# Gain vectors of the norms: multiplied into the weights at their split, instead of into the tokens

## The chip, the cores and the metric

One core of a Trainium2 chip runs the whole kernel. The metric is device time in microseconds (us) of one launch, lower is better; a measurement is the median of three runs. Times inside a launch come from one execution taken by the hardware profiler, counted from its first instruction.

Engines: PE multiplies matrices (PEld loads its weights), DVE works on vectors, ACT does copies with a scale and function tables, POOL is a second, slower vector engine, SP issues DMA requests. Every engine takes its own instructions strictly in order.

## The reference

One decoder layer on 1024 tokens of width 1024, in float32, with 256 memory tokens. Every RMS norm has a gain vector g:

```
def rms_norm(x, g):
    xf = x.astype(jnp.float32)
    y = xf * lax.rsqrt(jnp.mean(xf * xf, axis=-1, keepdims=True) + EPS)
    return (y * g.astype(jnp.float32)).astype(x.dtype)
...
  h = RMSNorm_pre(x); one combined input projection h @ w_in whose columns are
  partitioned into three head groups:
    A) dilated sliding-window causal attention (8 heads x 64, rotary) ...
    B) short gated convolution  B * conv3(C * v)  (256 channels = 4 groups x 64);
    C) cross-attention into memory tokens (4 heads x 64).
  each group output is RMS-normalised, groups are concatenated, one output
  projection, RMSNorm_post, residual add.  Then squared-ReLU MLP (4*D_MODEL)
  with pre/post RMSNorm and residual add.
```

A norm whose result goes only into a projection can be written in two ways: (x r g) W, or (x r) (g W), where r is the number per token and g is one number per row of W.

## The kernel before

Float32 products on PE are made of three. `split` (L88 to L92) cuts a tile in a high part (an ACT copy, names ending in h) and a low part (what is left, by a subtraction on DVE, or on POOL at L212); `mm3` then multiplies hi·hi (L101), lo·hi (L102) and hi·lo (L103) into one PSUM tile.

**Start, tokens.** Tokens come in 8 tiles of 128, then 2 of memory tokens (n = 0 to 9). For each: `x_sums` squares it on ACT with a running sum, and takes r on DVE (`ms`) and POOL (`rstd`); `x_norm` multiplies by r and by g, which is held on all 128 partitions, in one DVE instruction with two tensor inputs (`norm_to`, L138); `x_turn(n, q)` transposes half a tile on PE (L277) and splits it to hh and hl (mth and mtl for the memory tiles). `raw_mms(n, k0)` makes the products of tile n with two of the eight weight tiles. A block written out by hand (L547 to L640) sets the order of ACT, DVE, POOL and PE here: each tile's transposes stand between the products of the tile before.

**Weights.** `load_w` requests weight columns on SP, and `cut` splits one k tile of 128 rows into wh (ACT, L88) and wl (POOL, L212, or DVE). The weights of w_in come in four sets j = 0 to 3 (128 columns each of query, key and value) of eight k tiles; the set j = 0 lies in tiles named P at the start, its lo parts alternating between DVE and POOL, the others in `wraw` tiles, of which five exist, shared with the tokens. Behind them come the weights for the memory tokens' keys (wm) and values (wv), and later those of the other two groups. Each of them is split inside the stage before the one that uses it. For w_in sets with three column blocks, each request fetches one block for several k tiles.

**Gain loads.** The vector g_pre is fetched once to all partitions as 512 KB on SP in front of the first weights; g_mem and the gains of the three group outputs (g_y) likewise, later.

**Entry into attention (58 to 92 us).** `rope0` and `turn0` finish queries and keys of the first set, wm and wv are cut, the memory tiles are transposed and multiplied, and set j = 1 is cut for the first attention window, whose exponentials (L461) stand at its head. In each window the products of the next set fill PE between the attention's own steps.

**Outputs (403 to 445 us).** `y_norm` normalises the concatenated group outputs, `y_turn` transposes them (L929) and `wo_load` requests and splits the rows of w_out (woraw to oh and ol), the next request when an earlier lo part is done (`wo_low`). Meanwhile PE makes the last products of the convolution (`tail`), whose weights are the last `load_w`; `z`, `yc` and `yco` are its steps on DVE and ACT.

The rest, up to the end, is the MLP (from 560 us on), which the change doesn't touch.

Of the kernel before, what the change touches and what calls it, by code (L numbers as in the profile page):

```python
# [9 lines left out]
F = mybir.dt.float32  # L10
# [35 lines left out]
def hybrid_block(ctx, tc, x, mem, positions, g_pre_mix, g_mem, w_in, w_mem_kv, conv_w, g_attn_out,  # L46
# [40 lines left out]
    def copy(o, i, scale=1.0):  # L87
        nc.scalar.activation(o, i, AF.Copy, scale=scale)  # L88
# [85 lines left out]
    nc.scalar.activation(first, half_neg, AF.Square)  # L174
    cos = ac.tile([128, NS, 32], F, name="cos")
    sin = ac.tile([128, NS, 32], F, name="sin")

# [4 lines left out]
        XT[n] = stage(name="xt")  # L182
        nc.sync.dma_start(XT[n], tokens[n])

    def load_w(src, c0s, width, n_kt, get=None, later=None, engines=None):

        cols = width * len(c0s)
        engines = engines or [nc.gpsimd]
        res = []
        for k0 in range(0, KT, n_kt):  # L190
            if get and k0==0:
                load_gain(0, ac.tile([128, S], F, name="g_pre", tag="bias"), g_pre_mix)
            if get and k0 == KT // 2:
                load_x(1)
                nc.sync.dma_start(pos, positions[0].rearrange("(t p) -> p t", p=128))
                nc.sync.dma_start(invf, bass.AP(tensor=invf_in.tensor, offset=invf_in.offset,
                                                ap=[[0, 128], [1, 32]]))
            raw = get() if get else stage(name="wraw")
            rv = raw[:, :n_kt * cols].rearrange("p (k c) -> p k c", k=n_kt)
            for i, c0 in enumerate(c0s):  # L200
                nc.sync.dma_start(rv[:, :, i * width:(i + 1) * width],
                                  src[k0 * 128:(k0 + n_kt) * 128, c0:c0 + width].rearrange(
                                      "(k p) c -> p k c", p=128))
            for k in range(n_kt):
                wt = []
                res.append(wt)

                def cut(rv=rv, k=k, wt=wt, eng=engines[(k0 + k) % len(engines)]):
# [84 lines left out]
    nc.sync.dma_start(ident, ident_in)
    g_tok = {}

    def load_gain(n, dst, src):
        g_tok[n] = dst
        bcast_load(dst, src[0], 1024)
    cuts = []
    wj = load_w_in(0, get=lambda: pp.tile([128, 1024], F, name="P", tag="P", bufs=NP), later=cuts,  # L300
                   engines=[nc.vector, nc.gpsimd])
# [247 lines left out]
    with tc.manual_schedule(engines={ACT, DVE, POOL, PE}):  # L549
        ss = small.tile([128, 2], F, name="ss2", tag="ss2")  # L550
        for q in range(2):
            sumsq(ss[:, q:q + 1], XT[0][:, q * 512:(q + 1) * 512], 512)
        s1 = small.tile([128, 1], F, name="s1", tag="s1")
        nc.vector.tensor_add(s1, ss[:, 0:1], ss[:, 1:2])
        r = rstd(s1, D)
        tab = tables()
        for q in range(2):
            cl = slice(q * 512, (q + 1) * 512)
            norm_to(XT[0][:, cl], XT[0][:, cl], g_tok[0][:, cl], r)
        cuts.pop(0)()  # L560
        x_turn(0, 0)
        cuts.pop(0)()
        x_turn(0, 1)
        x_sums(1)
        cuts.pop(0)()
        cuts.pop(0)()
        x_norm(1)
        raw_mms(0, 0)
        cuts.pop(0)()
        cuts.pop(0)()  # L570
        raw_mms(0, 2)
        cuts.pop(0)()
        cuts.pop(0)()
        table_steps(2)
        x_turn(1, 0)
        raw_mms(0, 4)
        x_turn(1, 1)
        load_x(2)
        load_x(3)
        load_x(4)  # L580
        x_sums(2)
        table_steps(2)
        x_norm(2)
        raw_mms(0, 6)
        x_sums(3)
        for n in range(1, NS):
            if n + 4 < NS + 2:
                load_x(n + 4)
            if n == 4:
# [274 lines left out]
    g_y = gpool.tile([128, 1024], F, name="gy", tag="gain")  # L864
    bcast_load(g_y[:, 0:512], g_attn_out[0], 512)
    bcast_load(g_y[:, 512:768], g_conv_out[0], 256)
    bcast_load(g_y[:, 768:1024], g_xattn_out[0], 256)
# [7 lines left out]
    def y_norm(st, groups=((0, 512), (512, 256), (768, 256)), get=None):  # L875
# [660 lines left out]
```

## Time and profile before

| what | value |
|---|---|
| median of 3 runs | 1172.41 us (1171.89 to 1172.46) |
| profiled execution, its own time | 1171.13 us |
| its span, first to last instruction | 1169.3 us |
| mean granted clock of PE | 0.991 |
| busy: PE, DVE, ACT, POOL | 1124.3, 785.9, 622.7, 101.2 us |

Busy shares are means over stages that have different limits: PE is busy 96% of the span, so what is left to gain on it is some 45 us, spread over a few places. The time around the span (1171.13 against 1169.3) is launch and end.

### The profile page before, as it was taken

The numbers are of one execution on the slowest core, as the hardware profiler recorded it, in microseconds if no ns is written. First come the engines' busy times: TensorE is split into PE (matmuls) and PEld (weight loads), VectorE is DVE, ScalarE is ACT, GpSimd is POOL, SyncE is SP. The second block draws the span as 40 slices with busy tenths as digits, with TensorE's granted clock in tenths as the row PEclk, the third lists the DMA queues.
The fourth block names the chain that finished last, engine by engine and source line by source line (L and its number), as shares of the span: only waits on it lengthen the run. The fifth ranks groups of instructions, "written<-read, shape, count | busy, mean of one in ns | idle before, by whom it ended". The sixth has DMA issues, their size and how long they took to land.

```text
span 1169.3 us, 15898 instructions
## 1 busy us (share of the span) xinstructions
PE 1124.3 (96%) x5776; PEld 958.1 (82%) x5776; DVE 785.9 (67%) x1396; ACT 622.7 (53%) x1180; POOL 101.2 (9%) x129
## 2 busy tenths in 40 slices
PE   5979999999999999999999999999999999999996
PEld 4979989898888878887788888888888888888884
DVE  5977777676767356676866655665695565865776
ACT  5675666666667345554655545555654433434450
POOL 2270110202002021110000000000000000000001
PEclk9989999999999999999999999999999999999998
DMA  7341020100020454342474454445894465432205
GB/s 236 110 113 33 11 59 10 50 11 10 19 73 19 111 188 152 120 150 82 109 224 145 161 171 119 144 164 175 273 318 150 144 230 202 162 108 91 93 34 198
DMA packets 121310, 145.30 MB, mean 124 GB/s; under 512 B 8720, under 2 KB 74896, under 8 KB 121232
## 3 DMA queue, kind: packets, MB, share of 16 engines
q1 hardware_dynamic: 121232, 144.30, 37.8%
q8 instruction: 45, 0.74, 0.3%
q14 instruction: 33, 0.27, 0.1%
HBM read 102.33 MB, written 41.94 MB: 123 GB/s over the span
## 4 chain that ended last, share of the span: by engine, by line
PE 83%; DVE 7%; ACT 3%; DMA 3%; issue 2%; POOL 1%; SPq 1%; DVEq 0%; POOLq 0%; ACTq 0%
PE pt L1421 6%; PE mm L1421 6%; PE sc L1421 6%; PE mm L101 6%; PE mm L103 6%; PE mm L102 6%; PE tp L1421 3%; PE ot L1421 3%; PE sc L1132 2%; PE sc L1134 2%; PE mm L1132 2%; PE sc L1133 2%; PE mm L1134 2%; PE mm L1133 2%; PE pt L472 2%; PE sc L407 2%
## 5 line engine op out<-in xcount | busy, mean ns | idle before, releaser
L88 ACT ACTIVATE op<-fraw 128x1024 fp32r<-128x1024 f32 x56 | 59.3, 1059 | 147.5 <-PE tp L1421 75.7
L92 DVE TENSOR_TENSOR op<-fraw,op 128x1024 fp32r<-128x1024 f32 x56 | 68.5, 1223 | 92.4 <-ACT op L88 92.4
L130 POOL TENSOR_TENSOR rstd<-ms,half_neg 128x1 f32<-128x1 f32 (+2 forms) x43 | 29.4, 683 | 762.7 <-DVE s L1439 590.9
L101 PE MATMUL mm<-wh,hh 128*128 128x384 f32 x256 | 91.3, 356 | 0.8 <-ACT wh L88 0.8
L102 PE MATMUL mm<-wl,hh 128*128 128x384 f32 x256 | 87.2, 341 | 0.6 <-DVE wl L212 0.4
L103 PE MATMUL mm<-wh,hl 128*128 128x384 f32 x256 | 87.2, 341 | 0.0
L1421 PE MATMUL mm<-op 128*128 128x512 f32 x336 | 82.3, 395 | 2.5 <-DVE op L92 2.5
L212 POOL TENSOR_TENSOR wl<-wraw,wh 128x384 fp32r<-128x384 f32 (+1 forms) x62 | 56.5, 938 | 294.7 <-ACT wh L88 247.1
L1421 PE MATMUL pt<-op 128*128 128x512 f32 x336 | 80.7, 389 | 0.0
L1421 PE MATMUL sc<-op 128*128 128x512 f32 x336 | 80.4, 389 | 0.0
L1421 PEld LDWEIGHTS mm<-op 128*128 128x128 f32 x336 | 64.2, 191 | 16.4 <-DVE op L92 2.9
L1421 PEld LDWEIGHTS pt<-op 128*128 128x128 f32 x336 | 63.1, 188 | 13.1
L1421 PEld LDWEIGHTS sc<-op 128*128 128x128 f32 x336 | 63.1, 188 | 13.1
L92 DVE TENSOR_TENSOR tl<-pt,th 128x512 fp32r<-128x512 f32 (+1 forms) x96 | 60.0, 642 | 17.2 <-ACT th L88 16.5
L92 DVE TENSOR_TENSOR op<-r_b,op 128x1024 fp32r<-128x1024 f32 x56 | 68.2, 1218 | 0.8 <-ACT op L88 0.8
L461 ACT ACTIVATE P<-P,m 128x896 f32<-128x896 f32 (+3 forms) x64 | 49.7, 776 | 30.2 <-DVE m L459 29.5
L1116 ACT ACTIVATE ef<-ef 128x512 f32<-128x512 f32 x48 | 30.3, 631 | 63.5 <-DVE ef L1155 34.3
L88 ACT ACTIVATE th<-pt 128x512 fp32r<-128x512 f32 (+1 forms) x96 | 52.3, 560 | 20.0 <-PE pt L472 18.1
L88 ACT ACTIVATE op<-r_b 128x1024 fp32r<-128x1024 f32 x56 | 58.4, 1045 | 3.2 <-issue 3.2
L101 PE MATMUL mm<-hh,wh 128*128 128x512 f32 x128 | 52.0, 406 | 0.0
L103 PE MATMUL mm<-hh,wl 128*128 128x512 f32 x128 | 50.9, 398 | 0.0
L102 PE MATMUL mm<-hl,wh 128*128 128x512 f32 x128 | 50.7, 396 | 0.0
(345 smaller groups left out, 3072.5 us busy)
## 6 DMA issues: line engine op xcount, KB each, us to landing
wuraw<-in_w_up SPq DMA_DIRECT2D x32, 512.0 KB, 4.7
f_s<-ef SPq DMA_DIRECT2D x64, 256.0 KB, 2.1
r_b<-in_w_down SPq DMA_DIRECT2D x32, 512.0 KB, 4.8
fraw<-f_s SPq DMA_DIRECT2D x32, 512.0 KB, 3.7
f_a<-ef SPq DMA_DIRECT2D x48, 256.0 KB, 2.6
fraw<-f_a SPq DMA_DIRECT2D x24, 512.0 KB, 4.0
wraw<-in_w_in SPq DMA_DIRECT2D x60, 128.0 KB, 2.6
woraw<-in_w_out SPq DMA_DIRECT2D x8, 512.0 KB, 3.6
```

The costliest lines, as they stand in the source:

```text
L88: nc.scalar.activation(o, i, AF.Copy, scale=scale)
L92: nc.vector.tensor_sub(lo, src, hi.bitcast(F))
L101: nc.tensor.matmul(o, a_hi, b_hi, start=first, stop=False)
L102: nc.tensor.matmul(o, a_hi, b_lo, start=False, stop=False)
L103: nc.tensor.matmul(o, a_lo, b_hi, start=False, stop=last)
L212: eng.tensor_sub(wt[1][:, :cols], rv[:, k], wt[0][:, :cols].bitcast(F))
L461: nc.scalar.activation(p[:, :nk], p[:, :nk], AF.Exp, scale=-1.0, bias=m, accum_out=den[:, 2 * i + h:2 * i + h + 1])
L1116: nc.scalar.activation(t, t if src is None else src, AF.Relu)
L1132: nc.tensor.matmul(b, w[:, 0, k], th[:, k], start=(k == 0 and not prev), stop=False, skip_group_check=True)
L1133: nc.tensor.matmul(b, w[:, 0, k], tl[:, k], start=False, stop=False, skip_group_check=True)
L1134: nc.tensor.matmul(b, w[:, 1, k], th[:, k], start=False, stop=(k == 3), skip_group_check=True)
L1421: nc.tensor.matmul(b, x[:, k, cl], y[:, k], start=(first and s == 0 and k == 0 and m == 0), stop=(s == NSUB - 1 and k == 1 and m == 2), sk ...
```

## The change

No token is multiplied by a gain any more: `x_norm` and `y_norm` multiply by r alone, in an instruction with one tensor input (`scale_to`). The gain is multiplied into the weights where they are split. For that it is held as [128, 8], one column for each k tile of weights, fetched by requests on ACT's queue. In `cut` with a lo part on DVE, ACT's copy takes the column as its scale, and DVE's instruction multiplies and subtracts. With a lo part on POOL, ACT first scales the raw tile in place, and then copies it: one ACT instruction more per cut, 62 in all. For w_out, `wo_load` does as the DVE form does.

Further: the eight lo parts of the first w_in set are all on DVE, put off to places written out by hand (`lows`); w_in tiles are fetched by one request for each k tile, with its three column blocks; ident goes to ACT's queue; the first token tile's products are made with hi weights for all k (hi·hi and lo·hi), and the eight with wl come at the end; both transposes of tile 1 stand behind them.

```diff
+    def scale_to(t, r):
+        nc.vector.tensor_scalar(t, t, r, None, op0=OP.mult)
...
+        even = len(c0s) == 3 and c0s[2] - c0s[1] == c0s[1] - c0s[0] > 0
...
+            if even:
+                step = c0s[1] - c0s[0]
+                rows = src[k0 * 128:(k0 + n_kt) * 128, :3 * step].rearrange("(k p) (i c) -> p k i c", p=128, i=3)
+                for k in range(n_kt):
+                    nc.sync.dma_start(rv[:, k].rearrange("p (i c) -> p i c", i=3),
+                                      rows[:, k, :, c0s[0]:c0s[0] + width])
...
-                    copy(wt[0][:, :cols], rv[:, k])
-                    eng.tensor_sub(wt[1][:, :cols], rv[:, k], wt[0][:, :cols].bitcast(F))
+                    if eng is nc.gpsimd:
+                        copy(rv[:, k], rv[:, k], g)
+                        copy(wt[0][:, :cols], rv[:, k])
+                        eng.tensor_sub(wt[1][:, :cols], rv[:, k], wt[0][:, :cols].bitcast(F))
+                        return
+                    copy(wt[0][:, :cols], rv[:, k], g)
+
+                    def low():
+                        eng.scalar_tensor_tensor(wt[1][:, :cols], rv[:, k], g, wt[0][:, :cols].bitcast(F),
+                                                 op0=OP.mult, op1=OP.subtract)
...
     def x_norm(n):
-        norm_to(XT[n], XT[n], g_tok[n // NS], RS[n])
+        scale_to(XT[n], RS[n])
...
+            nc.scalar.dma_start(g_tok[n][:, k0:k0 + n_k], src[0].rearrange("(k p) -> p k", p=128))
...
-            mm3(p[:, :384], a, b, wj[k][0], wj[k][1], k == 0, k == KT - 1)
+            if n:
+                mm3(p[:, :384], a, b, wj[k][0], wj[k][1], k == 0, k == KT - 1)
+            else:
+                nc.tensor.matmul(p[:, :384], a, wj[k][0], start=(k == 0), stop=False)
+                nc.tensor.matmul(p[:, :384], b, wj[k][0], start=False, stop=False)
+        if n == 0 and k0 + 2 == KT:
+            for k in range(KT):
+                nc.tensor.matmul(p[:, :384], hh[:, k, st * 128:(st + 1) * 128], wj[k][1], start=False,
+                                 stop=(k == KT - 1))
...
-            norm_to(y[:, e0:e0 + wd], y[:, e0:e0 + wd], g_y[:, e0:e0 + wd], r[:, n:n + 1])
+            scale_to(y[:, e0:e0 + wd], r[:, n:n + 1])
...
-        copy(oh[:, k], raw)
-        lows.append(lambda: lo_part(ol[:, k], raw, oh[:, k]))
+        copy(oh[:, k], raw, gk)
+        lows.append(lambda: lo_part(ol[:, k], raw, oh[:, k], gk))
```

**DVE at the start.** These are DVE's rows from the first square sums on, before:

```order
L127 TENSOR_SCALAR ms<-s_137 128x1
L138 SCALAR_TENSOR_TENSOR xt<-xt,rstd,g_pre 128x512 x2
L212 TENSOR_TENSOR wl<-P,wh 128x384
L92 TENSOR_TENSOR hl<-pt,hh 128x4x128 x2
L127 TENSOR_SCALAR ms<-ss 128x1
L212 TENSOR_TENSOR wl<-P,wh 128x384
L138 SCALAR_TENSOR_TENSOR xt<-xt,rstd,g_pre 128x1024
L212 TENSOR_TENSOR wl<-P,wh 128x384 x2
```

And with the change (gt holds the gain's columns):

```order
L127 TENSOR_SCALAR ms<-s_133 128x1
L141 TENSOR_SCALAR xt<-xt,rstd 128x512 x2
L92 TENSOR_TENSOR hl<-pt,hh 128x4x128
L224 SCALAR_TENSOR_TENSOR wl<-P,gt_104,wh 128x384
L92 TENSOR_TENSOR hl<-pt,hh 128x4x128
L127 TENSOR_SCALAR ms<-ss 128x1
L224 SCALAR_TENSOR_TENSOR wl<-P,gt_104,wh 128x384 x3
L141 TENSOR_SCALAR xt<-xt,rstd 128x1024
L224 SCALAR_TENSOR_TENSOR wl<-P,gt_104,wh 128x384 x4
```

Eight lo parts stand on DVE where four stood, three of them ahead of tile 1's scaling; the token norms have lost their second tensor input.

**ACT at the entry into attention.** Before, around the last two copies of the memory tokens (mth):

```order
L88 ACTIVATE wh<-wraw 128x256 x2
L88 ACTIVATE mth<-pt 128x4x128
L88 ACTIVATE wh<-wraw 128x256 x2
L88 ACTIVATE mth<-pt 128x4x128
L88 ACTIVATE wh<-wraw 128x256 x4
L88 ACTIVATE QK<-sc 64x512 x2
```

With the change (gt_216 are the columns of g_mem, gt_104 those of g_pre):

```order
L88 ACTIVATE wraw<-wraw,gt_216 128x256
L88 ACTIVATE wraw<-wraw,gt_104 128x384
L88 ACTIVATE wh<-wraw 128x256
L88 ACTIVATE wh<-wraw,gt_216 128x256
L88 ACTIVATE mth<-pt 128x4x128
L88 ACTIVATE wraw<-wraw,gt_216 128x256
L88 ACTIVATE wraw<-wraw,gt_104 128x384
L88 ACTIVATE wh<-wraw 128x256
L88 ACTIVATE wraw<-wraw,gt_216 128x256
L88 ACTIVATE wh<-wraw 128x256
```

Between the copies stand scalings of the wm and wv tiles (256 wide) and, ahead of the memory tokens' last copies, already those of set j = 1 (384 wide), which need that set's data.

**ACT at the outputs.** Before, from the convolution's copy z on:

```order
L88 ACTIVATE z<-mm 128x512
L88 ACTIVATE wh<-wraw 128x256 x6
L88 ACTIVATE z<-mm 128x512
L88 ACTIVATE wh<-wraw 128x256 x2
L135 ACTIVATE sq,ssy<-y 128x512
L135 ACTIVATE sq,ssy<-y 128x256
L88 ACTIVATE oh<-woraw 128x1024 x2
```

With the change:

```order
L88 ACTIVATE z<-mm 128x512
L88 ACTIVATE wraw<-wraw,gt_104 128x256 x2
L88 ACTIVATE wh<-wraw 128x256 x2
L88 ACTIVATE wraw<-wraw,gt_104 128x256 x2
L88 ACTIVATE z<-mm 128x512
L88 ACTIVATE wh<-wraw 128x256 x2
L88 ACTIVATE wraw<-wraw,gt_104 128x256 x2
L88 ACTIVATE wh<-wraw 128x256 x2
L88 ACTIVATE wraw<-wraw,gt_104 128x256 x2
L88 ACTIVATE wh<-wraw 128x256 x2
L135 ACTIVATE sq,ssy<-y 128x512
L88 ACTIVATE oh<-woraw,gt_451 128x1024
```

Eight scalings stand between the copies, and the square sums of y behind them. On PE the transposes of y stand 16 products of `tail` in before, 41 in with the change.

## Rows read from the trace of the kernel before

**Rows 1.** Windows: busy time and instructions of each engine, then clock, DMA share, GB/s.
```profile
0.00:9.40 9.40, 0.02 (x1) 0.02 (x1) 1.20 (x5) 2.93 (x6) 0.75 (x5) 1.00 0.71 218
9.40:23.40 14.00, 10.25 (x46) 7.72 (x46) 11.67 (x18) 9.47 (x20) 6.32 (x6) 1.00 0.94 292
23.40:48.60 25.20, 25.16 (x160) 24.89 (x160) 21.48 (x51) 15.39 (x32) 2.70 (x5) 1.00 0.35 114
...
59.50:72.00 12.50, 6.76 (x35) 6.05 (x34) 12.28 (x21) 7.46 (x19) 9.97 (x15) 0.67 0.29 81
72.00:90.00 18.00, 16.72 (x123) 16.31 (x122) 11.35 (x25) 15.22 (x31) 12.50 (x14) 0.94 0.51 136
90.00:160.00 70.00, 67.85 (x470) 65.55 (x468) 49.17 (x136) 42.41 (x92) 7.95 (x8) 1.00 0.13 36
```

**Rows 2.** Waits of PE up to 100 us: in total, times, longest.
```profile
PE pt L277 <- DVE xt L138: 13.9, 4, 9.4
PE mm L102 <- DVE mtl L92: 2.1, 1, 2.1
PE sc L542 <- DVE qk L316: 1.5, 1, 1.5
...
PE pt L277 <- DVE ms L127: 0.6, 1, 0.6
```

**Rows 3.** Timeline of DVE, start: start, duration, idle before and its end.
```profile
5.40 0.15 DVE L127 TENSOR_SCALAR ms<-s 128x1 f32<-128x1 f32 x1
8.57 1.41 DVE L138 SCALAR_TENSOR_TENSOR xt<-xt,rstd,g_pre 128x512 f32<-128x512 f32 x2 [3.02 <-DMA P<-in_w_in]
10.35 0.56 DVE L212 TENSOR_TENSOR wl<-P,wh 128x384 fp32r<-128x384 f32 x1 [0.36 <-ACT wh L88]
...
14.50 2.07 DVE L138 SCALAR_TENSOR_TENSOR xt<-xt,rstd,g_pre 128x1024 f32<-128x1024 f32 x1
```

**Rows 4.** Timeline of SP's queue, ACT and PE at the start.
```profile
2.12 0.43 SPq L110 DMA_DIRECT2D g_pre<-in_g_pre_mix  x1
...
9.80 0.52 ACT L88 ACTIVATE wh<-P 128x384 fp32r<-128x384 f32 x1 [4.62 <-DMA P<-in_w_in]
...
12.43 1.06 ACT L135 ACTIVATE sq<-xt 128x1024 bf16<-128x1024 f32 x1 [0.40 <-DMA xt<-in_x]
...
23.43 0.63 PE L277 MATMUL pt<-ident,xt 128*128 128x128 f32 x4 [1.83 <-DVE xt L138]
```

**Rows 5.** DMA issues up to 60 us: KB, median us to landing.
```profile
g_pre<-in_g_pre_mix SPq DMA_DIRECT2D x1, 512.0 KB, 6.3
...
pos<-in_positions SPq DMA_DIRECT2D x1, 4.0 KB, 4.2
```

**Rows 6.** Groups of DVE up to 100 us, by shape: busy, mean ns.
```profile
L138 DVE SCALAR_TENSOR_TENSOR xt<-xt,rstd,g_pre 128x1024 f32<-128x1024 f32 x7 | 9.7, 1391 | 0.0
...
L245 DVE TENSOR_SCALAR tabI<-tabA 128x256 int32<-128x256 f32 x5 | 1.4, 284 | 0.0
```

**Rows 7.** Timeline of ACT, 58 to 92 us.
```profile
64.08 1.33 ACT L88 ACTIVATE wh<-wraw 128x256 fp32r<-128x256 f32 x4
...
84.42 1.35 ACT L88 ACTIVATE wh<-wraw 128x384 fp32r<-128x384 f32 x3
...
88.13 1.15 ACT L461 ACTIVATE P<-P,m 128x1024 f32<-128x1024 f32 x1
...
91.19 1.06 ACT L88 ACTIVATE th<-pt 128x512 fp32r<-128x512 f32 x2
```

**Rows 8.** Timeline at the outputs: POOL, ACT, PE, DVE.
```profile
408.64 5.67 POOL L212 TENSOR_TENSOR wl<-wraw,wh 128x256 fp32r<-128x256 f32 x8 [45.86 <-PE mm L103]
...
412.05 0.71 ACT L88 ACTIVATE wh<-wraw 128x256 fp32r<-128x256 f32 x2
...
415.82 0.87 PE L929 MATMUL pt<-ident,y 128*128 128x128 f32 x6 [1.56 <-DVE y L138]
...
421.14 0.49 DVE L804 TENSOR_SCALAR yc<-z,taps 128x512 f32<-128x512 f32 x1
```

More of the change, by code (lines that the diff above doesn't have):

```diff
@@ L173, in hybrid_block @@
     first = consts.tile([128, 1], F, name="first")
-    nc.scalar.activation(first, half_neg, AF.Square)
     cos = ac.tile([128, NS, 32], F, name="cos")
@@ L183, in load_x, with load_w @@
         nc.sync.dma_start(XT[n], tokens[n])
-    def load_w(src, c0s, width, n_kt, get=None, later=None, engines=None):
+    def load_w(src, c0s, width, n_kt, get=None, later=None, engines=None, fold=None, lows=None):
+        fold = g_tok[0] if fold is None else fold
+        even = len(c0s) == 3 and c0s[2] - c0s[1] == c0s[1] - c0s[0] > 0
         cols = width * len(c0s)
@@ L190, in load_w @@
         for k0 in range(0, KT, n_kt):
-            if get and k0==0:
-                load_gain(0, ac.tile([128, S], F, name="g_pre", tag="bias"), g_pre_mix)
-            if get and k0 == KT // 2:
+            if get and k0 == n_kt:
                 load_x(1)
-                nc.sync.dma_start(pos, positions[0].rearrange("(t p) -> p t", p=128))
-                nc.sync.dma_start(invf, bass.AP(tensor=invf_in.tensor, offset=invf_in.offset,
-                                                ap=[[0, 128], [1, 32]]))
             raw = get() if get else stage(name="wraw")
             rv = raw[:, :n_kt * cols].rearrange("p (k c) -> p k c", k=n_kt)
-            for i, c0 in enumerate(c0s):
+            if even:
[4 more added lines that the diff above has]
+                                      rows[:, k, :, c0s[0]:c0s[0] + width])
+            for i, c0 in enumerate(c0s if not even else ()):
                 nc.sync.dma_start(rv[:, :, i * width:(i + 1) * width],
@@ L206, in load_w, with cut @@
                 res.append(wt)
-                def cut(rv=rv, k=k, wt=wt, eng=engines[(k0 + k) % len(engines)]):
+                def cut(rv=rv, k=k, wt=wt, eng=engines[(k0 + k) % len(engines)], g=fold[:, k0 + k:k0 + k + 1]):
                     wt.append(pw.tile([128, 384], R, name="wh", tag="wh", bufs=8))
                     wt.append(pw.tile([128, 384], R, name="wl", tag="wl", bufs=8))
-                    copy(wt[0][:, :cols], rv[:, k])
-                    eng.tensor_sub(wt[1][:, :cols], rv[:, k], wt[0][:, :cols].bitcast(F))
+                    if eng is nc.gpsimd:
[7 more added lines that the diff above has]
+                                                 op0=OP.mult, op1=OP.subtract)
+                    if lows is None:
+                        low()
+                    else:
+                        lows.append(low)
                 if later is None:
@@ L290, in hybrid_block, with load_gain @@
     XT[0] = stage(name="xt")
+    g_tok = {}
+    def load_gain(n, rows):
+        g_tok[n] = consts.tile([128, KT], F, name=f"gt{n}")
+        k0 = 0
+        for src in rows:
+            n_k = src.shape[1] // 128
+            nc.scalar.dma_start(g_tok[n][:, k0:k0 + n_k], src[0].rearrange("(k p) -> p k", p=128))
+            k0 += n_k
+    load_gain(0, [g_pre_mix])
+    nc.scalar.dma_start(ident, ident_in)
+    nc.scalar.activation(first, half_neg, AF.Square)
     for q in range(2):
         nc.sync.dma_start(XT[0][:, q * 512:(q + 1) * 512], tokens[0][:, q * 512:(q + 1) * 512])
[L293 to L301, printed above, removed]
+    cuts, lows = [], []
+    wj = load_w_in(0, get=lambda: pp.tile([128, 1024], F, name="P", tag="P", bufs=NP), later=cuts, lows=lows,
+                   engines=[nc.vector])
+    nc.sync.dma_start(pos, positions[0].rearrange("(t p) -> p t", p=128))
+    nc.sync.dma_start(invf, bass.AP(tensor=invf_in.tensor, offset=invf_in.offset, ap=[[0, 128], [1, 32]]))
     QT, VT = {}, {}
@@ L522, in raw_mms @@
             a, b = hh[:, k, st * 128:(st + 1) * 128], hl[:, k, st * 128:(st + 1) * 128]
-            mm3(p[:, :384], a, b, wj[k][0], wj[k][1], k == 0, k == KT - 1)
+            if n:
+                mm3(p[:, :384], a, b, wj[k][0], wj[k][1], k == 0, k == KT - 1)
+            else:
+                nc.tensor.matmul(p[:, :384], a, wj[k][0], start=(k == 0), stop=False)
[4 more added lines that the diff above has]
+                                 stop=(k == KT - 1))
         if k0 + 2 == KT:
@@ L556, in hybrid_block @@
         tab = tables()
[L557 to L564, printed above, removed]
         cuts.pop(0)()
         cuts.pop(0)()
+        for q in range(2):
+            scale_to(XT[0][:, q * 512:(q + 1) * 512], r)
+        x_turn(0, 0)
+        lows.pop(0)()
+        cuts.pop(0)()
+        raw_mms(0, 0)
+        x_turn(0, 1)
+        cuts.pop(0)()
+        raw_mms(0, 2)
+        x_sums(1)
+        lows.pop(0)()
+        lows.pop(0)()
+        cuts.pop(0)()
+        lows.pop(0)()
         x_norm(1)
-        raw_mms(0, 0)
+        cuts.pop(0)()
+        raw_mms(0, 4)
+        lows.pop(0)()
         cuts.pop(0)()
         cuts.pop(0)()
[L571 to L577, printed above, removed]
+        lows.pop(0)()
+        lows.pop(0)()
+        lows.pop(0)()
         load_x(2)
@@ L580, in hybrid_block @@
         load_x(4)
+        load_gain(1, [g_mem])
+        raw_mms(0, 6)
+        x_turn(1, 0)
+        x_turn(1, 1)
+        table_steps(2)
         x_sums(2)
@@ L583, in hybrid_block @@
         x_norm(2)
-        raw_mms(0, 6)
         x_sums(3)
@@ L589, in hybrid_block @@
             if n == 4:
-                load_gain(1, kv.tile([128, S], F, name="g_mem", tag="QK", bufs=NSETS), g_mem)
+                load_gain(2, [g_attn_out, g_conv_out, g_xattn_out])
             if n == 6:
                 cuts = []
-                wm = load_w(w_mem_kv, [0], 256, 4, later=cuts, engines=[nc.gpsimd, nc.gpsimd, nc.gpsimd, nc.vector])
+                wm = load_w(w_mem_kv, [0], 256, 4, later=cuts, engines=[nc.gpsimd, nc.gpsimd, nc.gpsimd, nc.vector],
+                            fold=g_tok[1])
             raw_mms(n, 0)
@@ L630, in hybrid_block @@
         cuts = []
-        wv = load_w(w_mem_kv, [256], 256, 4, later=cuts)
+        wv = load_w(w_mem_kv, [256], 256, 4, later=cuts, fold=g_tok[1])
         turn0(0)
@@ L863, in hybrid_block @@
     w = load_w(w_in, [U0 + 128, B0 + 128], 128, 4)
[L864 to L867, printed above, removed]
     YS, YP, OB, XR = {}, {}, {}, {}
@@ L905, in wo_load @@
         nc.sync.dma_start(raw, w_out[k * 128:(k + 1) * 128])
-        copy(oh[:, k], raw)
-        lows.append(lambda: lo_part(ol[:, k], raw, oh[:, k]))
+        gk = g_tok[2][:, k:k + 1]
+        copy(oh[:, k], raw, gk)
+        lows.append(lambda: lo_part(ol[:, k], raw, oh[:, k], gk))
     def wo_low():
```

## The prediction

> **What bounds the kernel now.** I read the windows first. From 90 us on PE is busy 67.85 of 70 us in an attention window, and before that it is short in three stretches: 0.02 of 9.4 us, 10.25 of 14.0 us up to 23.4, and 6.76 of 12.5 plus 16.72 of 18.0 between 59.5 and 90 [rows 1]. In the same rows the reader sees who is busy there instead: DVE 11.67 of 14.0 before 23.4, DVE 12.28 of 12.5 before 72, and ACT 15.22 of 18.0 behind it. The waits of PE name the instruction: 13.9 us on token norms, 9.4 of them before its first instruction and 1.8 and 2.1 later, then 2.1 on the low part of the memory tokens, 1.5 on a rotation and 0.6 behind `ms` [rows 2, 4]. All of that is DVE. In the first of the late stretches PE was granted 0.67 of its clock on average, a mix of its two levels of 1.2 and 2.4 GHz, after idling for 5.7 us in it [rows 1]; what less idle would give back there I leave in the bounds. So a change that makes DVE's norms cheaper works where PE waits; one that gives ACT more works where ACT has little left between 59.5 and 90.
>
> **The start.** The norm of tile 0 began at 8.57 after 3.02 us of idle, though `ms` was done at 5.55; the row puts the idle down to a DMA on SP's queue [rows 3], and of the norm's operands that is g_pre, requested at 2.12 and 6.3 us under way [rows 4, 5]. Without it r is ready some 0.6 us after `ms`, and two scalings of 512 follow, 0.49 each by the only one-tensor row of that width [rows 8]. The first transposes then start near 7 instead of 9.4. The columns of g are 1024 words of 4 bytes, as pos is, which landed in 4.2 us [rows 5]; issued first, on ACT's queue, they are there by 6, ahead of the first weights.
>
> But 2.4 us at the head are not 2.4 us at 23.4. ACT's first wh waited for P until 9.80, and the square of tile 1 stood at 12.43 behind its own DMA [rows 4]; both move only by what g_pre's 512 KB took of a DMA that is 71 to 94% busy [rows 1], under 2 us, and the squares stand in ACT's order behind three weight copies and two hh. Then DVE: the change takes from it, up to the norm of tile 2, 1.41 + 2.07 + 1.39 = 4.87 us of norms [rows 3, 6] and puts 0.98 + 0.9 + 0.9 there, where 0.9 for a width of 1024 is an estimate that continues 0.284 at 256 and 0.49 at 512 [rows 6, 8]. That is 2.1 less. It adds four low parts that POOL had, 0.56 each [rows 3]: 2.2 more. DVE has the same work as before, in a stretch where it is the busiest engine. I walk the new order with these durations: the last low part of tile 0 near 18, tile 1's transposes done at 19.2, tile 2's norm and first transposes at 22.9 instead of 23.43. **Gain 0.5**; bounds 0.5 lost (the squares of tile 1 late by one more copy) and 1.9 won (the whole 1.83 us wait of the row).
>
> **Up to 59.5.** PE runs without a gap from 23.4 to 48.6, DVE is busy 21.48 of 25.2 [rows 1]. Seven norms of 1.39 become 0.9, so DVE gets ahead, and the one wait of PE behind it, 0.6 at tile 7, goes [rows 2]. **Gain 0.6**, bounds 0 and 1. The gain requests on ACT's queue and the joint w_in requests cost nothing seen here: the first fall in ACT's idle time (15.39 busy of 25.2) and the second move the same bytes; if that cover is gone, a request costs ACT what one costs SP, 0.43 [rows 4].
>
> **Entry into attention.** On DVE three norms fall into its full stretch, each 0.5 shorter: up to 1.5 us earlier for the memory tiles and so for 2.1 + 2.1 + 1.5 of PE's waits [rows 2]. On ACT 14 scalings of 256 and 8 of 384 come in. A copy of these widths goes at 1.33/4 = 0.33 and 1.35/3 = 0.45 [rows 7]. A scale by partition isn't in the trace; the nearest pair is an exponential of 1024 with a bias by partition, 1.15 us [rows 7], against 1.06 for a plain 1024 square [rows 4], so 0.09 more. That makes 14 x 0.42 + 8 x 0.54 = 10.2 us; without the 0.09, 8.2. ACT's idle in 59.5 to 90 is 5.04 + 2.78 = 7.8 [rows 1]. ACT is then full, with 2.4 us left over, and in its strict order set j = 1 is scaled ahead of memory copies and must wait for its data, 0.7 and 1.4 us by my walk. Behind it stand the exponentials and th, 91.19 before [rows 7], on which the first window's products end. PE has cover for part: set j = 1 of weights is for later products, and DVE's 1.5 us come in front. I take **0.8 lost**, between 1.5 won (DVE's part passes through, ACT's surplus hides in the window, where ACT is busy 42.41 of 70) and 4.4 lost (2.4 + 2.1 with nothing won).
>
> One rule of the chip speaks against DVE's part. In the row at 14.50 a norm with two tensor inputs took 2.07 beside POOL, against the mean of 1.39 [rows 3, 6]: 0.7 more, shared reading. The Trainium skill ("SBUF — State Buffer", Who interferes with whom) says more of the new form: a `tensor_scalar` in a two-port mode and GpSimd exclude each other for whole instructions. The trace of before has no 1024-wide scaling beside POOL to show it.
>
> **The other sets.** For j = 2 and 3 eight scalings each, 8 x 0.54 = 4.3 us, fall in windows where ACT is busy 42.41 of 70 and PE idle 2.15 [rows 1]. They can only delay an in-order th by one copy. **0.2 lost**, bounds 0 and 1. Each later weight load has the same cover.
>
> **Outputs.** PE waited 1.56 at 415.82 for the norm of y; that norm stood behind POOL's `rstd`, and this behind eight low parts, 408.64 to 414.31 [rows 8]. Eight scalings of 0.42 come into ACT, 3.4 us, while it waits part of this time for weights; the last copies ended at 412.76 [rows 8], and I get 414.3 and POOL's end 1.6 later. The norm itself gets 0.2 shorter. PE no longer waits there, since the transposes stand 25 products later, 25 x 0.23 (estimate: 5.7 us of cover). But `rstd`, the low parts of w_out and so its next requests, which wait for them in turn, come 1.6 to 3 us later, and yc and yco stand behind them on DVE and ACT. 1.56 won against 2.2 lost: **0.6 lost**, bounds 1.6 won and 3 lost.
>
> **Sum.** -0.5 - 0.6 + 0.8 + 0.2 + 0.6 = +0.5 us, on 1171.13 of the profiled execution: 1171.6. The median of the runs is 1172.41, 1.3 above, so I give 1172.9. A measurement here tells about 0.2%, 2.35 us, from no change; this is **no change**.
>
> **Rivals.** *Faster:* ACT's scalings hide, so that DVE's 1.5 us pass through at the entry, and y's wait is gone without a later one, 1 us won. -0.5 - 0.6 - 1.5 + 0.2 - 1.0 = -3.4: 1169.0. For it: all of PE's waits are on DVE, and ACT's idle of 7.8 is near the 8.2 of scalings without the 0.09. Against: the order puts scalings in front of memory copies. *Slower:* ACT is the bound at the entry. -0.5 - 0.6 + 4.4 + 0.2 + 0.6 = +4.1: 1176.5. It decides from the point where th comes more than 2.5 us later than 91.19 at PE's pace. For it: 10.2 us into 7.8. *The late gain was not what held the start* (weights and squares do): the first term is 0, 1173.4. *Lock:* if each scaling beside POOL waits for one of its low parts, two memory norms cost 0.9 + 0.8 instead of 1.36; DVE loses 0.7 in place of 1.0 won, the sum is +2.2, 1174.6; POOL's row at the entry is busy 9.97 of 12.5 [rows 1], which speaks for it, and the scalings of 256 at a mean of 0.284 [rows 6] against it, though few lay beside POOL's work. That is the rule of the page above.
>
> **Chances.** Forecast 0.36, no gain at the start 0.07, lock 0.06, faster 0.28, slower 0.23. The first three lie within 2.35 us, but for some 0.05 at their ends, which I share out: faster by over 0.2% 0.30, within 0.2% 0.44, slower 0.26. The range leaves out 2 in 10: from a little below the faster rival, 1168.2, to the slower one's 1176.5.
>
> **What would show it.** First transposes near 7, tile 2's near 22.9, and no POOL work of weights before 24. No wait of PE near 49. Norms of 1024 at 0.9; 0.4 would be a faster scaling, above 1.3 beside POOL the lock. Between 59.5 and 90 ACT busy over 29 of 30.5, its scalings at 0.42 and 0.54, and th at 91 to 92. At the outputs POOL's last weight near 416, no wait at the transposes of y, a new one at the convolution's. I am wrong on the faster side if ACT's waits at the entry turn out to be idle time that PE does not miss, and on the slower if the set j = 1 arrives so late that ACT stands still in front of the memory copies.

## The result, and the profile after

The changed kernel took 1180.72 us (median of 4 runs, 1177.71 to 1181.75) against 1172.15 of the kernel before (4 runs): a ratio of 1.0071, 95% interval 1.0051 to 1.009. It is slower by some 8 us, where no change was forecast and the range ended at 1176.5. The profiled execution took 1181.75, with a span of 1179.9 against 1169.3. It is the longest of the four, 1.0 above their median, so its places add up to more than 8 us.

Where the time went is found with the starts of the same instructions in both traces (PE's transposes of tile 2, ACT's first th of the attention, its first exponential of the gathered heads, and its 17th copy yh; us from the span's start):

| kernel | tile 2 | first th | gathered heads | yh, 17th |
|---|---|---|---|---|
| before | 23.4 | 91.2 | 340.5 | 520.1 |
| changed | 25.1 | 94.7 | 347.4 | 531.3 |
| late by | 1.7 | 3.5 | 6.9 | 11.2 |

So four places lose: the start 1.7, the way to the first th 1.8 (2.3 counted from tile 7, where the start's loss had shrunk to 1.2), the windows up to 340 us 3.4, and the outputs 4.3. From there on both kernels run alike, and 0.6 comes back.

These sizes are those of one execution of each kernel. The kernels of the experiments share most of the changed code, so their profiles tell how steady a place is. With the changed start, tile 2 came at 24.3 to 25.8. With all scalings at the entry, the way from tile 7 to the first th took 0.8 to 2.3 longer than before. With the last weights scaled on ACT in the changed order, the outputs lost 4.2 to 5.4. The windows are the uneven place: 3.1 of the lateness arise between 318 and 356 us here, and only 0.7 to 1.1 in five other kernels with the same scalings there.

The windows of the changed kernel, as [rows 1], with three around 337 and at 450 us added:

```profile
9.40:23.40 14.00, 12.01 (x42) 9.57 (x42) 8.46 (x18) 7.87 (x17) 0.85 (x1) 1.00 0.87 238
23.40:48.60 25.20, 23.49 (x150) 23.20 (x151) 19.74 (x53) 14.56 (x30) 3.29 (x6) 1.00 0.33 100
...
59.50:72.00 12.50, 9.06 (x57) 8.16 (x56) 10.52 (x21) 10.29 (x24) 9.17 (x13) 0.86 0.34 105
72.00:90.00 18.00, 15.55 (x105) 13.23 (x104) 11.24 (x25) 16.29 (x35) 8.57 (x12) 1.00 0.23 68
...
330.00:337.20 7.20, 4.96 (x32) 4.12 (x31) 1.79 (x8) 5.10 (x14) 0.00 (x0) 1.00 0.60 164
337.40:340.60 3.20, 3.20 (x17) 3.10 (x16) 0.93 (x4) 2.81 (x8) 0.00 (x0) 0.50 0.00 0
...
450.00:453.20 3.20, 2.63 (x10) 2.26 (x11) 1.67 (x5) 2.24 (x8) 0.36 (x2) 0.50 0.62 243
```

At the entry ACT is busy 26.6 of 30.5 us (22.7 before), DVE has eased, and PE's granted clock is higher than before (0.86 and 1.00 against 0.67 and 0.94). At 337 and 450 PE is granted half its clock, 1.2 GHz, each time with a wait. For the start the clock column reads 1.00 in both kernels, but there products of 384 columns follow each other at 0.32 us up to 18 us, against 0.17 later, so I go by that spacing. The waits of PE, in total, times and longest, beside [rows 2]:

```profile
PE pt L294 <- DVE xt L141: 8.9, 2, 8.0
...
PE pt L970 <- DVE y L141: 4.1, 1, 4.1
PE ot L509 <- ACT th L88: 3.9, 6, 2.2
...
PE pt L294 <- DVE ms L127: 1.8, 1, 1.8
PE mm L102 <- DVE mtl L92: 1.4, 1, 1.4
```

The norms' waits have shrunk from 13.9 to 8.9, but 1.8 for tile 2's norm now stand behind `ms` (0.6 before), so 3.8 are gone. New are 4.1 on the second half of y and 2.2 of the 3.9 on th. The start, on PE and then ACT (answers to [rows 4]):

```profile
8.02 1.12 PE L294 MATMUL pt<-ident,xt 128*128 128x128 f32 x4 [8.02 <-DVE xt L141]
...
17.87 0.52 PE L554 MATMUL mm<-wh,hl 128*128 128x384 f32 x1
18.19 2.31 PE L557 MATMUL mm<-wl,hh 128*128 128x384 f32 x8
20.34 1.03 PE L294 MATMUL pt<-ident,xt 128*128 128x128 f32 x8
...
25.11 0.63 PE L294 MATMUL pt<-ident,xt 128*128 128x128 f32 x4 [1.78 <-DVE ms L127]
```
```profile
5.71 0.63 ACT L135 ACTIVATE sq<-xt 128x512 bf16<-128x512 f32 x1 [1.35 <-DMA xt<-in_x]
...
20.98 1.10 ACT L88 ACTIVATE hh<-pt 128x512 fp32r<-128x512 f32 x2
21.95 1.07 ACT L135 ACTIVATE sq<-xt 128x1024 bf16<-128x1024 f32 x1
```

The transposes of tile 1 stand at 20.34, behind all 24 products of tile 0; ACT's copies of them at 20.98; and behind these, in ACT's order, the square of tile 2 that its norm needs. ACT around 334 us, and PE there:

```profile
333.57 1.13 ACT L88 ACTIVATE wraw<-wraw,gt 128x384 f32<-128x384 f32 x2 [1.62 <-DMA wraw<-in_w_in]
...
335.51 0.62 ACT L88 ACTIVATE wraw<-wraw,gt 128x384 f32<-128x384 f32 x1 [0.43 <-DMA wraw<-in_w_in]
336.15 0.60 ACT L88 ACTIVATE th<-pt 128x512 fp32r<-128x512 f32 x1
```
```profile
336.80 0.39 PE L509 MATMUL ot<-th,V 128*128 128x256 f32 x1 [2.24 <-ACT th L88]
```

ACT waits for the convolution's weights in order to scale them, while the copy th that PE needs stands behind. And the outputs, POOL, ACT, DVE and PE in turn (answers to [rows 8]):

```profile
418.58 4.28 POOL L219 TENSOR_TENSOR wl<-wraw,wh 128x256 fp32r<-128x256 f32 x6 [0.86 <-ACT wh L88]
424.71 0.71 POOL L130 TENSOR_TENSOR rstd<-ms,half_neg 128x2 f32<-128x2 f32 x1 [1.85 <-DVE ms L127]
```
```profile
422.11 1.14 ACT L88 ACTIVATE oh<-woraw,gt 128x1024 fp32r<-128x1024 f32 x1
423.15 0.40 ACT L135 ACTIVATE sq<-y 128x256 bf16<-128x256 f32 x1
...
438.01 1.16 ACT L88 ACTIVATE oh<-woraw,gt 128x1024 fp32r<-128x1024 f32 x1 [6.19 <-DMA woraw<-in_w_out]
```
```profile
423.28 1.28 DVE L94 SCALAR_TENSOR_TENSOR ol<-woraw,gt,oh 128x1024 fp32r<-128x1024 f32 x1 [0.89 <-ACT oh L88]
424.48 0.15 DVE L127 TENSOR_SCALAR ms<-ssy 128x1 f32<-128x1 f32 x1
```
```profile
450.57 0.66 PE L970 MATMUL pt<-ident,y 128*128 128x128 f32 x2 [4.10 <-DVE y L141]
```

POOL's last low part ends at 422.9, in the stage's own time (6.9 us late as a whole) 1.7 later than before; `rstd` stands 3.5 later, the later requests of w_out 3, and the second half of y, which needs the convolution behind them, lets PE wait 4.1 us. It is not POOL that held `rstd`: POOL stood idle for 1.85 us in front of it, waiting for `ms`. On ACT a copy of w_out stood between the two square sums of y, and on DVE the low part of that copy stood ahead of the second `ms`.

### The profile page after: what moved, and what is told of

Read it like the earlier page. It is cut to its first block, busy times and chain, and to the rows that moved or that the text cites. A ratio compares the mean times of both kernels' runs of the same rounds, so it can differ in the third digit from the quotient of the medians.

```text
span 1179.9 us, 15906 instructions
## 1 busy us (share of the span) xinstructions
PE 1132.4 (96%) x5776; PEld 961.6 (81%) x5776; DVE 776.9 (66%) x1400; ACT 654.5 (55%) x1242; POOL 97.1 (8%) x125
## 4 chain that ended last, share of the span: by engine, by line
PE 82%; DVE 6%; ACT 6%; issue 2%; DMA 2%; POOL 1%; SPq 0%; POOLq 0%; ACTq 0%; DVEq 0%
PE pt L1462 6%; PE mm L1462 6%; PE mm L103 6%; PE mm L102 6%; PE mm L101 6%; PE sc L1462 6%; PE tp L1462 3%; PE ot L1462 3%; PE sc L1173 2%; PE mm L1173 2%; PE sc L1174 2%; PE sc L1175 2%; PE mm L1175 2%; PE mm L1174 2%; PE pt L499 2%
## 5 line engine op out<-in xcount | busy, mean ns | idle before, releaser
L101 PE MATMUL mm<-wh,hh 128*128 128x384 f32 x248 | 87.9, 355 | 0.3 <-ACT hh L88 0.3
L102 PE MATMUL mm<-wl,hh 128*128 128x384 f32 x248 | 84.6, 341 | 1.1 <-POOL wl L219 1.1
L103 PE MATMUL mm<-wh,hl 128*128 128x384 f32 x248 | 84.0, 339 | 0.1
```

Of the source, the lines that this page charges most:

```text
L101: nc.tensor.matmul(o, a_hi, b_hi, start=first, stop=False)
L102: nc.tensor.matmul(o, a_hi, b_lo, start=False, stop=False)
L103: nc.tensor.matmul(o, a_lo, b_hi, start=False, stop=last)
```

## The experiments

Each was timed beside the kernel before, and ratios are to it. Theory: ACT's 62 in-place scalings lose the time, at three places, and the start's order the rest. Rivals stand with each.

**No scalings.** Whether ACT's added instructions are the cause at all.

```diff
-                        copy(rv[:, k], rv[:, k], g)
```

> The changed kernel without ACT's 62 in-place scalings (the gain is left out of all weights whose low part is made on POOL; the rest is as changed). Theory 'ACT's scalings': three places of the changed profile lose 2.3 us (entry, 59 to 92), 3.0 us (at 334) and 4.3 us (outputs), all behind these instructions; without them about 1171 to 1172.5, and the start's 1.7 us is all that stays against the kernel before, less what DVE's shorter norms won. Rival 'order and start': the new product order, the request form and the start shift the whole program, and the scalings only fill idle time of an engine that is 55% busy; then 1178 or more.

0.9992 (0.9983 to 1.0001), 1170.83 us. The 62 instructions cost 0.8%; without them the change would have made no difference, and the rival falls. The start stays late (tile 2 at 24.5).

**One place at a time.** The same line is left out for one load of weights (`pre` guards it): the last, the convolution's, and those cut at the entry.

```diff
-    w = load_w(w_in, [U0 + 128, B0 + 128], 128, 4)
+    w = load_w(w_in, [U0 + 128, B0 + 128], 128, 4, pre=False)
```
```diff
-    w = load_w(w_in, [U0, B0, C0 + 128], 128, 2)
+    w = load_w(w_in, [U0, B0, C0 + 128], 128, 2, pre=False)
```
```diff
-                            fold=g_tok[1])
+                            fold=g_tok[1], pre=False)
...
-        wv = load_w(w_mem_kv, [256], 256, 4, later=cuts, fold=g_tok[1])
+        wv = load_w(w_mem_kv, [256], 256, 4, later=cuts, fold=g_tok[1], pre=False)
...
-        wj = load_w_in(j + 1, later=cuts)
+        wj = load_w_in(j + 1, later=cuts, pre=j > 0)
```

> The changed kernel without the eight in-place scalings of the last weights alone (U0 + 128, B0 + 128; their gain is left out). Theory 'ACT's scalings': POOL's low parts end about 3 us sooner in the stage, rstd and the requests of w_out move with them, the wait of 4.1 us at the transposes of y shrinks below 1.5, no drop of PE's clock behind it: 1176 to 1177.5. Rival 'order': y's normalisation stands behind two low parts of w_out on DVE and the transposes stand later in any case; then the wait stays over 3 us and the time at 1179.5 to 1181.5.

> The changed kernel without the in-place scalings of the eight convolution weights at 328 to 340 alone (U0, B0, C0 + 128; their gain is left out). Theory 'ACT waits in order': a scaling waits for its weights' transfer (1.6 and 0.4 us) ahead of the copy th that PE waits for (2.2 us), and PE then runs 3.4 us at half its clock; without it 3 us less, 1177 to 1178.5, no wait of PE over 0.6 there and no lower clock at 337. Rival 'load': it is ACT's added busy time (4.3 us in 12), and half the gain comes; 1179 to 1180.

> The changed kernel without the in-place scalings of wm, wv and the set j = 1, 22 instructions between 59 and 100 us (their gain is left out). Theory 'ACT full': the first th comes 2.3 us sooner against the start, at about 92.4, and the whole is 2 to 2.5 us shorter: 1178 to 1178.8. If DVE's shorter norms pass through as well, 3.5 less: 1177. Rival 'later slack': the stage's gain is given back in the windows, where PE waits for th anyway; 1180 to 1181.

Ratios 1.0033 (1.002 to 1.0046), 1.0044 (1.0031 to 1.0058) and 1.0046 (1.0033 to 1.0058): each place alone gives back 0.25 to 0.4%, together 0.9%, about what all at once gave. The first is clear of the changed kernel's interval; the other two overlap it, so their sizes are rough. Without the last weights' scalings the waits of PE on y are (outputs, total and longest):

```profile
PE pt L971 <- DVE y L141: 1.9, 1, 1.9
PE tp L865 <- DVE yc L859: 1.5, 1, 1.5
```

not 4.1, though not below the 1.5 that I had set, and PE's clock does not drop; `rstd` follows POOL's last low part at once there. Without the convolution's, no wait of PE is left between 300 and 345 us, and between 318 and 356 us 0.9 is gained on the kernel before. Where those scalings stay, the place is milder than in the profile above. Here is the kernel without the last weights' scalings, its wait and its window:

```profile
PE ot L510 <- ACT th L88: 1.4, 1, 1.4
```
```profile
330.00:345.00 15.00, 13.53 (x81) 10.66 (x79) 7.81 (x23) 10.34 (x27) 0.00 (x0) 1.00 0.27 74
```

In five such profiles the wait is 1.2 to 1.6 us, PE keeps its full clock, and 0.7 to 1.1 are lost. The mechanism is the same, the 3.1 is that execution's. Without the entry's, the first th comes at 93.4, of which the start of that execution had 0.6 more than the changed kernel's: 1.9 better.

**A warm PE.** The start showed products at 0.32 us each up to 18 us, against 0.17 at full clock; I took the early start of a PE with little to do for the cause of the 1.7.

```diff
+        warm = pt_bank()
+        for i in range(24):
+            nc.tensor.transpose(warm[:, i % 4 * 128:(i % 4 + 1) * 128], ident, ident)
         x_turn(0, 0)
```

> The changed kernel with 24 transposes of ident into an unused bank on PE ahead of the first token transposes, which nobody reads. In the changed profile PE starts at 8.0, stands still between short pieces of work, and its products of 384 columns follow each other at 0.32 us up to 18 us, against 0.17 from 12.6 us on before. Theory 'clock': with PE busy from about 4.5 us on, the full clock comes before 12, tile 0's products take 0.17, tile 2's first transposes come at 23.4 to 24 instead of 25.1, and the whole is 1 to 2 us shorter: 1179 to 1179.7. Rival 'chain': ACT's and DVE's order sets the start (copies, square of tile 1, low parts), products only get shorter, and tile 2's transposes stay within 0.4 us of 25.1: 1180.3 to 1181.

1.0071 (1.0058 to 1.0083). On PE:

```profile
5.82 4.36 PE L598 MATMUL pt<-ident 128*128 128x128 f32 x24 [5.82 <-DMA ident<-in_ident]
10.01 0.60 PE L294 MATMUL pt<-ident,xt 128*128 128x128 f32 x4
...
12.30 0.34 PE L553 MATMUL mm<-wh,hh 128*128 128x384 f32 x1
12.47 0.34 PE L554 MATMUL mm<-wh,hl 128*128 128x384 f32 x1
...
25.08 0.63 PE L294 MATMUL pt<-ident,xt 128*128 128x128 f32 x4 [1.78 <-DVE ms L127]
```

The products do follow at 0.17, and tile 2 comes at 25.08 all the same; the time is the changed kernel's. So the theory's forecast fell. But the run is no clean test of the clock: the useless transposes kept PE until 10.0, and tile 0's own came 2.0 later than in the changed kernel. What the shorter products won may have gone there.

Other profiles say that PE's pace has a part. The kernel before with only its later low parts on DVE (below) has before's start, the same instructions in the same order. In its profile products stand 0.32 apart up to 19.4, where they stood 0.17 apart before, and tile 2 comes 1.2 later than before's 23.43:

```profile
18.78 0.52 PE L101 MATMUL mm<-wh,hh 128*128 128x384 f32 x1
19.10 0.52 PE L102 MATMUL mm<-wl,hh 128*128 128x384 f32 x1
...
24.66 0.63 PE L277 MATMUL pt<-ident,xt 128*128 128x128 f32 x4 [1.86 <-DVE xt L138]
```

And with the changed start tile 2 comes at 24.3 where the last eight products of tile 0 took 1.76 us, and at 25.8 where they took 2.77. So some of the 1.7 is PE's pace; how much stays open. The next experiment changes the order alone.

**The start's order of before**, with the fold and eight low parts on DVE.

```diff
-        raw_mms(0, 6)
-        x_turn(1, 0)
-        x_turn(1, 1)
+        x_turn(1, 0)
+        raw_mms(0, 4)
+        x_turn(1, 1)
...
+        raw_mms(0, 6)
```

> The changed kernel with the start's order of before (three products for each k, tile 1's transposes between them, each low part at once, all eight on DVE). Theory 'clock': PE's work is denser at its start, so the full clock comes at about 13; but DVE has all eight low parts ahead of tile 1's norm. Tile 2's transposes at 23 to 24.3; the whole 1 to 2 us shorter, 1178.7 to 1179.7. Rival 'the new order is right for these low parts': PE waits for each wl in turn, 25 or later, 1180.5 to 1182.

1.0032 (1.002 to 1.0043): 0.4% better, more than expected. On PE and ACT:

```profile
14.79 1.05 PE L294 MATMUL pt<-ident,xt 128*128 128x128 f32 x4
...
17.43 0.60 PE L294 MATMUL pt<-ident,xt 128*128 128x128 f32 x4
...
21.48 0.63 PE L294 MATMUL pt<-ident,xt 128*128 128x128 f32 x4 [1.37 <-DVE xt L141]
```
```profile
18.59 1.06 ACT L135 ACTIVATE sq<-xt 128x1024 bf16<-128x1024 f32 x1
```

Here, too, the products of 384 run at 0.32 up to 17 us. Tile 1's transposes between them bring the square of tile 2 from 21.95 to 18.59, and tile 2 to 21.48: 3.6 earlier than changed, 2.0 earlier than before.

**Low parts on DVE**, all of them by multiply and subtract: no in-place scaling.

```diff
-        engines = engines or [nc.gpsimd]
+        engines = [nc.vector]
```

> The changed kernel with every low part of weights on DVE (copy with the scale on ACT, multiply and subtract on DVE), so no in-place scaling and nothing on POOL; the result is whole. Theory 'ACT's scalings': ACT has as many instructions as before the change, the three places recover as without scalings, less what DVE's 62 instructions of 0.5 to 0.6 us cost where it is full (at the entry 22 of them, 11 us, into some 8.7 us of idle time): 1172 to 1175. Rival 'any added instruction in order': DVE becomes at the entry and at the outputs what ACT was; 1177 to 1181.

0.9967 (0.9955 to 0.9978), faster than the kernel before, where at best its time was expected. With the edits of the last two experiments together:

> The start's order of before and every low part of weights on DVE, in the changed kernel; the result is whole. Theory 'two separate losses' (tile 1's transposes put behind all of tile 0's products; ACT's scalings): the gains add, 3.6 us of the start on top of what the low parts on DVE gave, a ratio of about 0.9935 to the kernel before, 1164 to 1165.5 beside 1171.5. Rival 'one slack': the start's gain is met again at the entry, where DVE is full with 22 more low parts, and the ratio stays at 0.996 to 0.9975.

0.991 (0.9896 to 0.9923), 1161.76 us against 1172.56: the gains add, with a little on top (the changed kernel's ratio less both gains is 0.9928), and this is the best version, with tile 2 at 21.1, the first th at 88.5 and yh at 512.5.

**The same without the fold.** Whether the fold earned this. The kernel before, with its low parts on DVE, first without and then with those of the first set:

```diff
-        engines = engines or [nc.gpsimd]
+        engines = engines if get else [nc.vector]
```
```diff
-        engines = engines or [nc.gpsimd]
+        engines = [nc.vector]
```

> The kernel before, with the low parts of all weights but the first set on DVE instead of POOL, nothing folded. It tells whether the gain of the low parts on DVE comes from the fold. Theory 'fold': DVE still has the norms with two tensor inputs at the entry, and its 22 more low parts make it late: slower than before, 1172.5 to 1175. Rival 'POOL was slow': the gain is of the low parts alone (0.6 us on DVE against 1.0 on POOL): 0.997 of before or less, 1167 to 1169.

> The kernel before with all low parts of weights on DVE, those of the first set too, nothing folded. Beside the kernel with the fold, the start's order of before and all low parts on DVE (0.991) it differs in the fold and the way of its loads alone. Theory 'the fold is worth something where ACT is spared': the norms stay at 1.4 us and behind g_pre's load, DVE has 2.2 us more at the start than before, tile 2's transposes come at 24.5 or later, 0.995 to 0.998 of before. Rival 'it is all the low parts' engine': 0.990 to 0.993, tile 2's transposes at 22 or earlier.

0.9956 (0.9943 to 0.997) and 0.9945 (0.9932 to 0.9959). So more than half of the best version's gain needs no fold. The fold with its loads is the rest, 0.9945 against 0.991, some 4 us; 2.4 of them stand at tile 2 already (23.5 against 21.1). The first theory falls for the larger part, and my 24.5 for tile 2 was a miss.

**POOL scales.**

```diff
-                        copy(rv[:, k], rv[:, k], g)
+                        nc.gpsimd.tensor_scalar(rv[:, k], rv[:, k], g, None, op0=OP.mult)
```

> The changed kernel with the 62 in-place scalings on POOL instead of ACT; the result is whole. POOL is busy 8% in all, but 17.7 of 30.5 us at the entry and 5.8 us of eight low parts at the outputs, and wh on ACT must now wait for POOL's scaling. Theory 'ACT in order': the place at 334 recovers (3 us), since a wait for the weights' transfer holds POOL and not the copies th. At the entry and the outputs POOL's chain gets longer by 0.6 to 0.8 us a weight: no gain there. 1176 to 1179. Rival 'whoever scales, the weights are late': 1180 to 1186.

1.03 (1.0286 to 1.0314). Groups of POOL there (busy, mean ns, idle before):

```profile
L217 POOL TENSOR_SCALAR wraw<-wraw,gt 128x384 f32<-128x384 f32 x40 | 49.4, 1250 | 46.4 <-DMA wraw<-in_w_in 46.0 <-PE pt L103 0.3
L219 POOL TENSOR_TENSOR wl<-wraw,wh 128x384 fp32r<-128x384 f32 x40 | 39.9, 1022 | 160.5 <-ACT wh L88 160.2
```

I had put a scaling at 0.6 to 0.8; it takes 1.25. The first th comes 21.6 us later than in the changed kernel, and the wait on th at 334 is gone (longest 0.4): locally as expected, in sum far off, beyond the rival's range too.

**Requests of before.**

```diff
-        even = len(c0s) == 3 and c0s[2] - c0s[1] == c0s[1] - c0s[0] > 0
+        even = False
```

> The changed kernel with the three requests for two k tiles again in place of one for each k tile. My prediction counted the joint request at nothing. If so: the ratio of the changed kernel, 1.007, within 0.15%. Rival 'requests': the joint form lands each k tile later or earlier than the scheduler takes it; over 0.2% from 1.007, either way.

1.0059 (1.0046 to 1.0072), within the bound, and the intervals overlap: no difference that can be told.

**Scaling second**, behind the copy, so that the first instruction needs a free wh tile.

```diff
-                        copy(rv[:, k], rv[:, k], g)
-                        copy(wt[0][:, :cols], rv[:, k])
+                        copy(wt[0][:, :cols], rv[:, k], g)
+                        copy(rv[:, k], rv[:, k], g)
```

> The changed kernel with the two ACT instructions of a cut in the other order: wh is copied from the raw tile with the scale, and then the raw tile is scaled in place for POOL. As many instructions of ACT, the result whole; but the first of them now needs a free wh tile, so that it no longer stands early in ACT's order, where it waits for the weights' transfer ahead of th. Theory 'place in the order': the wait at 334 goes, 3 us or more come back, and the entry loses less: ratio 1.001 to 1.004, 1173 to 1176. Rival 'busy time': ACT has the same 31 us more, ratio 1.006 to 1.008.

1.0071 (1.0058 to 1.0083): no gain. The place at 334 did recover (between 318 and 356 us this kernel gains 0.6 on the one before, where the changed one loses 3.1 and others like it 0.7 to 1.1). But the scaling now stands between wh and the low part, and PE waits for that from 90 to 300 us:

```profile
PE mm L102 <- POOL wl L219: 5.3, 9, 1.5
PE mm L103 <- POOL wl L219: 1.7, 3, 1.1
```

(0.9 in the changed kernel), which gives some 2 us away, and the outputs lose 5.8. In this order the scalings cost in other places, and as much.

## Why the prediction was wrong

Forecast was 0.5 us lost, measured were some 8. The sum's terms for the start (0.5 won), the other sets (0.2 lost) and the outputs (0.6 lost) failed, and the entry's was too small.

**What bounds the kernel: right.** DVE's norms were what PE waited for, and their waits shrank by 3.8 us.

**The start: wrong in a step.** "I walk the new order": tile 1's transposes done at 19.2, tile 2 at 22.9. They ended at 21.4, and tile 2 came at 25.1 (24.3 to 25.8 over the profiles with this start). DVE's load was right (9.7 us busy up to 23.4 there; low parts 0.55 apart, four of them and not three ahead of tile 1's scaling, the 1024-wide scaling at 0.75 rather than 0.9), though its last low part of tile 0 ended at 19.45 and not near 18. But DVE was not the end of the chain. The square of tile 2 was: it stands on ACT behind tile 1's copies, these behind PE's last product of tile 0. I had priced the moved transposes and not what is queued behind them on ACT. The order of before, with the same low parts, is 3.6 better. The walk also had no term for PE's pace: products stood 0.32 apart up to 18.2, and some of the 1.7 may be that. That the first transposes came at 8.0 and not at 7 was one transfer: the second half of tile 0's tokens, for whose square ACT waited until 5.71.

**Up to 59.5: right.** Predicted 0.6 won; the lateness falls from 1.7 to 1.2.

**Entry: mechanism right, size too small.** The prices held: 0.50 for a scaling of 256 columns and 0.61 for one of 384, against 0.41 and 0.52 for plain copies, the 0.09 of the estimate. ACT was not full as forecast, 26.6 of 30.5 us against over 29: it waited in between. I took 0.8 lost of a range up to 4.4, counting DVE's 1.5 in front; 2.3 were lost (0.8 to 2.3 over the profiles with this entry), and leaving out the scalings gave some 0.25% back. Without any scalings the same way took 1.2 less than before, so DVE's part did pass through, and the scalings cost 2.0 to 3.5. ACT's own waits there:

```profile
65.62 0.62 ACT L88 ACTIVATE wraw<-wraw,gt 128x384 f32<-128x384 f32 x1 [0.59 <-DMA wraw<-in_w_in]
...
70.33 0.62 ACT L88 ACTIVATE wraw<-wraw,gt 128x384 f32<-128x384 f32 x1 [0.43 <-POOL qk L343]
...
77.40 0.62 ACT L88 ACTIVATE wraw<-wraw,gt 128x384 f32<-128x384 f32 x1 [1.36 <-DVE KS L428]
...
94.69 0.60 ACT L88 ACTIVATE th<-pt 128x512 fp32r<-128x512 f32 x1 [0.65 <-PE pt L499]
```

**The other sets: a step that failed.** "Each later weight load has the same cover", from a mean idle share of ACT, with 0.2 lost. Idle time is no cover for an instruction that waits in order: the scaling waited 1.6 and 0.4 us for its transfer with th behind it, PE stood for 2.2, and then ran 3.2 us or more at half its clock. That made most of the 3.4 lost in the windows of that execution; five other profiles lost 0.7 to 1.1 at this place, with shorter waits and no fall of the clock. A mean over a window cannot show this; the order showed it, and I had read it at the entry and the outputs alone.

**Outputs: the largest miss.** POOL's end 1.7 later and no wait at the first transposes of y came as written, and the wait moved to the convolution's half. But the chain that I priced, POOL's low parts and then `rstd`, did not hold `rstd`. The scalings pushed y's square sums back on ACT, a copy of w_out came between them and its low part ahead of `ms` on DVE, and POOL waited for that 1.85 us. ACT's order, shown ahead of the prediction, has that copy behind the first square sum; I read only the scalings in it. The same gap stands in five other profiles with these scalings. I set 2.2 lost against 1.56 won; it was 4.1 of new waiting and 3.2 us or more at half clock with it: 4.3 in all instead of 0.6, and 4.2 to 5.4 in those five. Leaving out eight scalings took that wait to 1.9.

**Rivals.** *Slower* had the engine right and only one of its places. *Lock* did not come: no 1024-wide norm took over 0.75. Around the norm at the entry, on DVE and POOL:

```profile
60.93 0.75 DVE L141 TENSOR_SCALAR xt<-xt,rstd 128x1024 f32<-128x1024 f32 x1
60.98 1.01 POOL L342 TENSOR_TENSOR qk<-yo,tmp 128x128 f32<-128x128 f32 x1 [0.69 <-PE sc L577]
```

The POOL row took 1.01 beside it, and 0.52 at 69.24 without one. If there was a lock, POOL paid; the Trainium skill ("SBUF — State Buffer", Who interferes with whom) says that whoever issues first holds the port, and one overlap agrees with that without showing it.

What stays open: how much of the start's loss is PE's pace, how the outputs' loss splits between ACT's copies and DVE's low parts of w_out that stand ahead of y's norm, and how the best version's 0.35% from the fold splits beyond the start.

## What to carry to other kernels

An instruction added to an engine that is half idle is priced by what stands behind it in that engine's order and by what it waits for, place by place; a mean of idle time says nothing on either. When a step is moved, follow each of its successors on every engine, not the busiest alone. And before a factor is folded into another operand, ask which instruction can carry it: here it cost 0.06 us in a low part of 384 columns, as the multiply of a multiply and subtract on DVE, and 0.8% of the whole as a pass of its own on ACT.

## What the runs showed of the hardware

- With waits of 2.24 and 4.10 us PE was granted 0.50 of its clock, 1.2 GHz, from 337.4 to 340.6 and from 450.0 to 453.2. With waits of 1.2 to 1.6 us at the first of these places, in five other profiles, it kept its full clock.
- A low part of 384 columns took 0.61 us on DVE with the multiplication in it, 0.55 without, and 1.02 on POOL; POOL's scaling of the same tile took 1.25, ACT's 0.61.
- Useless transposes ahead of tile 0 brought PE's products from 0.32 to 0.17 us apart at 12.3 us, held its first useful work back by 2.0 us, and tile 2 came no earlier (25.08 against 25.11).
